# Down-projection operands of a Strassen-style product, made one at a time, in a two-layer encoder kernel

## The chip, the cores and the metric

The kernel runs on one core of a Trainium2 chip. The metric is device time in microseconds (us) of one execution; times of several executions are summed up by their median. The engines that matter are TensorE (PE, matmuls), VectorE (DVE), ScalarE (ACT), GpSimd (POOL) and SyncE (SP), whose queue issues most transfers from HBM.

## The reference, cut to what matters

Two request groups of 512 tokens with 1024 features (float32) go through two layers with shared weights. Each layer is an attention block with four kinds of heads and then a gated MLP with 2816 hidden features. The part at hand is the end of the MLP:

```
u = h @ w_up
up = jnp.pad(u, ((0, 0), (1, 1), (0, 0)))
u = up[:, :-2] * conv_w[0] + up[:, 1:-1] * conv_w[1] + up[:, 2:] * conv_w[2] + conv_b
val, gate = jnp.split(u, 2, axis=-1)
return (val * jax.nn.silu(gate)) @ w_down
```

The result, times a gate per feature, is added to the residual x. The product with `w_down` (2816 x 1024) for both request groups is the down projection.

## The kernel before, in words

**Precision.** Every float32 product is made of three matmuls (`mm3`, L162 to L164). An operand is split into a high half, a rounded copy that ACT makes (L1082), and a low half, operand minus high half, a 128x512 subtract of two SBUF operands (L1078 through `minus`, on DVE or POOL). In the trace the high halves of weights are tiles `whi`, the low halves `wlo`; those of activations are `hh` and `hl`. The pool `hp` has 16 buffers `hh` and 16 `hl`; in the down projection these buffers also hold the raw gated activations as they come from HBM (`g_raw`: `hh` for request group 0, `hl` for request group 1).

**Seven products in place of eight.** The hidden features are 22 chunks of 128 (f = 0 to 21). The down projection takes them in groups of 2n chunks, with n = 3, 3, 3 in layer 0 (`P['gr']`; its last four chunks are multiplied plainly) and n = 4, 3, 4 in layer 1. A group is a 2x2 block product (halves of the features, halves of the output columns, two request groups), done by a Strassen-Winograd scheme with seven products. Each is n x 4 x 3 matmuls: 36 for n = 3, 48 for n = 4. We call them P1 to P7, and a group "first", "second", "third" within its layer. P1 and P2 take raw blocks, P3 to P7 combinations. For each of the n pairs of chunks, `w_combos` makes four sums or differences of weight blocks and `g_combos` four of activation blocks, so 24 of them for n = 3 and 32 for n = 4, and each operand of each product is split, seven weight and seven activation splits for each pair. The temporaries `s1` and `t1` take buffers of the tag `td`, 6 in layer 0 and 8 in layer 1, which is exactly one group's need; they are read last by the split for P4.

**Order.** Both helpers are Python generators. For each product the loop calls `next` on every one of them, then emits the product's matmuls. The third call, ahead of P3, made all four combinations of a pair at once. The compiler orders the instructions of each engine by this order as priority and by its own estimate of when operands are ready; on the chip each engine then takes its list strictly in order. After each product four `add_x` instructions on DVE (L1290) add a PSUM bank to x.

**Who does what.** Strings in `P` give the engine, 'v' for DVE and 'p' for POOL, in turn. `'dl': 'vvp'` are the low halves in the down projection, one in three on POOL. `'ds'` and `'db'`, both 'p', are the weight and activation combinations of all groups but a layer's first; `'d0': 'v'` and `'d1': 'p'` those of the first.

**Weights in flight.** `down_raw` loads one chunk of `w_down` (512 KB) into a ring of buffers: `fr` (letter x, 4 in layer 0, 6 in layer 1, shared with the up projection) and then `fs` (letter d, 3, in memory that is freed when the up projection's temporaries are gone), so 7 and 9 buffers. A group wants 6 or 8 chunks. `sa` is a ring of buffers of the same size (4 in layer 0, 2 in layer 1) for modulation weights, used only up to the end of the up projection.

The up projection uses the same scheme and the same `w_combos`, with other engine keys (`'us'` on POOL, `'ul'` on DVE).

Of the kernel before, what the change touches and what calls it, by code (L numbers as in the profile page):

```python
# [8 lines left out]
F32 = mybir.dt.float32  # L9
# [16 lines left out]
EPS = 1e-6  # L26


P = {'w0': 2.41, 'w1': 2.07, 'b0': 1.49, 'j0': 1.86, 'j1': 1.0, 'p0': 1.06, 'p1': 0.83, 'v': 0.29, 'vd': 0.32, 'f': 0.13, 'fc': 1.16, 'm0': 2.02, 'm1': -0.42, 'o0': 0.58, 'o1': 0.68, 'o2': 0.44, 'a0': 0.66, 'a1': 3.46, 'S': 7, 'K': 6, 'R': 2, 'e': 'p', 'q': 'aa', 'r': 'pv', 'pd': 0.07, 's': -0.28, 'we': 'vvp', 'x': [4, 5, 6, 7, 13, 15, 17, 19], 'hl': 'vpvpvvvv', 'ul': 'v', 'us': 'p', 'ug': 'p', 'uc': 'v', 'uf': 'p', 'tb': 'vpv', 'tl': 'vvvp', 'ds': 'p', 'db': 'p', 'dl': 'vvp', 'ft': [9, 10], 'td': [6, 8], 'fr': [4, 6], 'fs': 3, 'na': 6, 'n1': 2, 'n2': 2, 'gr': [[3, 3, 3], [4, 3, 4]], 'd0': 'v', 'd1': 'p', 't0': 4, 't1': 25, 'sa': [4, 2], 'at': [3.2, 21.2], 'ag': [[4, 4, 0], []]}
UNITS = ['C0', 'D0', 'C2', 'A0', 'D1', 'C1', 'B1', 'A1', 'B0']  # L30
CHUNK = {"A0": 0, "A1": 1, "B0": 2, "B1": 3, "C0": 4, "C1": 5, "C2": 6, "D0": 7, "D1": 8}
GSCALE = {"A": 64 ** -0.5, "B": 64 ** -0.5, "C": 64 ** -0.5, "D": 32 ** -0.5}
# [36 lines left out]

XPOS = P['x']  # L70

# [5 lines left out]
def trunk_kernel(tc, xT, cT, w_ada, w_adac, b_ada, norm_g, w_in, w_out, w_out2, w_out9, w_up, w_down, conv, qkn, rpb,  # L77
                 amask, t5, onehot, tmask, sink, lam_d, subln, blk, ident_in, out):
    nc = tc.nc
    with ExitStack() as ctx:  # L80
# [55 lines left out]
        class Weights:  # L136
# [10 lines left out]
            def split(self, s, cols):  # L147
                hi = self.pool.tile([128, self.width], F32R, name="whi", tag="whi", bufs=self.ring)
                lo = self.pool.tile([128, self.width], F32R, name="wlo", tag="wlo", bufs=self.ring)
                nc.scalar.activation(hi[:, :cols], s[:, :cols], AF.Copy)  # L150
                self.count += 1
                self.eng[self.count % len(self.eng)].tensor_tensor(lo[:, :cols], s[:, :cols], hi[:, :cols].bitcast(F32), op=ALU.subtract)  # L152
                return hi, lo
# [157 lines left out]
        with tc.tile_pool(name="pa", bufs=1, reuse_waits="tile") as pa, \  # L311
# [6 lines left out]
            e = px.tile([128, KC, NG], F32, name="e_c", bufs=1)  # L318
# [57 lines left out]
            for g in range(NG):  # L376
# [3 lines left out]
                for k in range(KC):  # L380
                    hi = hp.tile([128, T], F32R, name="hh", tag="hh")
                    lo = hp.tile([128, T], F32R, name="hl", tag="hl")
# [61 lines left out]
        for l in range(DEPTH):  # L444
# [3 lines left out]
            with ExitStack() as at_ctx:  # L448
# [592 lines left out]
                o0, o1 = outproj(0), outproj(1)  # L1041
# [18 lines left out]
            with ExitStack() as ff_ctx:  # L1060
                fx = ff_ctx.enter_context(tc.tile_pool(name=f"fx{l}", bufs=1, reuse_waits="tile"))
                raws = lambda: fx.tile([128, 1024], F32, name="fr", tag="fr", bufs=P['fr'][l])
# [14 lines left out]
                def minus(key, o, a, b):  # L1077
                    pick(key).tensor_tensor(o, a, b, op=ALU.subtract)  # L1078
# [12 lines left out]
                def w_split(key, s, extra=False):  # L1091

                    blocks, c = [], 0
                    if extra:
                        return quarters(split(key, s, tuple(fx.tile([128, T], F32R, name=n, tag=n, bufs=1)
                                                            for n in ("xhi", "xlo"))))
                    while c < T:
                        if not tail:
                            tail.extend([tuple(W.pool.tile([128, W.width], F32R, name=n, tag=n, bufs=W.ring)
                                               for n in ("whi", "wlo")), 0])  # L1100
                        t, o = tail
                        n = min(T - c, W.width - o)
                        tail.clear()
                        if o + n < W.width:
                            tail.extend([t, o + n])
                        p = split(key, s[:, c:c + n], tuple(x[:, o:o + n] for x in t))
                        blocks += [tuple(x[:, i:i + 128] for x in p) for i in range(0, n, 128)]
                        c += n
                    return blocks

                def w_combos(key, lo, a, tmp):

                    a11, a12, a21, a22 = a
                    yield w_split(lo, a11)
                    yield w_split(lo, a12)
                    s1 = tmp("s1")
                    plus(key, s1, a21, a22)
                    minus(key, a21, a11, a21)
                    minus(key, a11, s1, a11)
                    minus(key, a12, a12, a11)  # L1120
                    for s in (a11, s1, a21, a12, a22):
                        yield w_split(lo, s)

                mm_last[0] = None

# [27 lines left out]
                sa_tile = lambda: fx.tile([128, D], F32, name="sa", tag="sa", bufs=P['sa'][l])  # L1153
# [10 lines left out]
                t0, t1 = P['at']  # L1164
# [18 lines left out]
                with tc.tile_pool(name=f"ft{l}", bufs=1, reuse_waits="tile") as fp, \  # L1183
# [3 lines left out]
                    ft = lambda name: fp.tile([128, T], F32, name=name, tag="ft", bufs=P['ft'][l])  # L1187
# [22 lines left out]
                    us = [t[:, j * T:(j + 1) * T] for t in (sa_tile(), sa_tile()) for j in range(2)]  # L1210
# [26 lines left out]
                    for f in range(NC1, NF):  # L1237
# [11 lines left out]
                        s1 = copy(a)  # L1249
# [17 lines left out]
                fd = ff_ctx.enter_context(tc.tile_pool(name=f"fd{l}", bufs=1, reuse_waits="tile"))  # L1267
                nt = lambda name: fd.tile([128, T], F32, name=name, tag="nt", bufs=3)
                td = lambda name: fd.tile([128, T], F32, name=name, tag="td", bufs=P['td'][l])
                rings = itertools.cycle("x" * P['fr'][l] + "d" * P['fs'])  # L1270

                def down_raw(f):
                    s = raws() if next(rings) == "x" else fd.tile([128, 1024], F32, name="fs", tag="fs", bufs=P['fs'])
                    dma(s, w_down[l, :, f * 1024:(f + 1) * 1024])
                    return s

# [7 lines left out]
                def g_pair():  # L1284
                    return tuple(hp.tile([128, T], F32R, name=n, tag=n) for n in ("hh", "hl"))
# [9 lines left out]
                def g_combos(key, lo, b):  # L1295

                    b11, b12, b21, b22 = b
                    yield split(lo, b11, g_pair())
                    yield split(lo, b21, g_pair())
                    t1 = td("t1")  # L1300
                    minus(key, t1, b12, b11)
                    minus(key, b12, b22, b12)
                    minus(key, b11, b22, t1)
                    minus(key, b21, b21, b11)
                    for s in (b11, t1, b12, b22, b21):
                        yield split(lo, s, g_pair())

                def four(k):
                    return [p_mm(), p_sc(), p_mm(), p_sc()] if k % 2 else [p_tp(), p_pp(), p_tp(), p_ov()]
# [2 lines left out]
                for gi, n in enumerate(P['gr'][l]):  # L1312
                    rw, rg = [], []
                    for i in range(n):
                        rw.append(down_raw(f0 + i))
                        rg.append(g_raw(f0 + i))
                    for i in range(n, 2 * n):
                        rw.append(down_raw(f0 + i))
                        rg.append(g_raw(f0 + i))
                    if gi == 0:  # L1320
                        xs = [(fe if g else fd).tile([128, KC, T], F32, name=f"x{g}", bufs=1) for g in range(NG)]
                        for g, j in ((0, 0), (1, 0), (1, 4), (0, 4)):
                            dma(xs[g][:, j:j + 4], x_ap[:, g, j:j + 4])
                    qa = [w_combos('ds' if gi else 'd0', 'dl', (rw[i][:, :512], rw[n + i][:, :512], rw[i][:, 512:], rw[n + i][:, 512:]), td)
                          for i in range(n)]
                    qb = [g_combos('db' if gi else 'd1', 'dl', rg[i] + rg[n + i]) for i in range(n)]
                    a, b = four(gi + 1), four(gi)
                    c = b
                    for bi, (bank, start, outs) in enumerate(((a, True, ((0, 0),)), (b, True, ((0, 0),)), (a, False, ((1, 0),)),
                                              (c, True, ((1, 4),)), (a, False, ((1, 4),)), (c, False, ((1, 0),)),  # L1330
                                              (a, False, ((0, 4),)))):
                        A = [next(q) for q in qa]
                        B = [next(q) for q in qb]
                        with tc.issue_after(mm_last[0]):
                            pairs = [(i, dp) for i in range(n) for dp in range(4)]
                            if l + 1 == DEPTH and bi == 6:
                                pairs.sort(key=lambda p: p[1])
                            for i, dp in pairs:
                                ins = mm3(bank[dp], A[i][dp], B[i], start and i == 0, i == n - 1)
                        mm_last[0] = ins  # L1340
                        for dp in range(4):
                            for g, d0 in outs:
                                add_x(g, d0 + dp, bank[dp])
                                if f0 + 2 * n == NF and bi in (1, 4, 5, 6) and (dp % 2 or bi == 6):
                                    o = slice(d0 + dp - (bi < 6), d0 + dp + 1)
                                    dma(out[:, g, o], xs[g][:, o])
                    f0 += 2 * n
# [3 lines left out]
                for f in range(f0, NF):  # L1351
                    s = down_raw(f)
# [128 lines left out]
```

## Time and profile before

| what | us |
|---|---|
| median of 3 runs | 2802.25 (2798.87 to 2803.78) |
| the profiled execution | 2799.13 |
| its span, first to last instruction | 2797.3 |
| PE busy in the span | 2610.4 |

The span is 1.8 us shorter than that execution's own time; the rest lies around it. PE's ends are modelled, so its busy time is no measure of full speed; the argument goes by the starts of matmuls and by how long a stage lasts against the number of its matmuls. The down projection begins at about 1209.6 us (layer 0) and 2544.9 us (layer 1) of the span.

### The profile page before, as it was taken

How to read it: one execution, taken by the hardware profiler on the slowest of the kernel's cores; microseconds unless marked ns; L12 is line 12 of the kernel's file. 1: busy time of each engine (PE TensorE's matmuls, PEld its weight loads, DVE VectorE, ACT ScalarE, POOL GpSimd, SP SyncE). 2: the span in 40 equal slices, each digit the busy share in tenths (PEclk: the TensorE clock that was granted, in tenths of full speed). 3: DMA queues.
4: the chain of work that ended last, by engine and by line, in shares of the span. 5: the costliest groups of instructions: out<-in, count | busy, mean ns of one | idle time of the engine just before them, and what ended most of it. 6: DMA issues, size and time to landing. Idle time of an engine off the chain costs nothing. (4 is left out here: it accounts for less than half of the span.)

```text
span 2797.3 us, 39805 instructions
## 1 busy us (share of the span) xinstructions
PE 2610.4 (93%) x13612; PEld 2207.7 (79%) x13612; DVE 2066.3 (74%) x4004; ACT 1393.3 (50%) x2970; POOL 1217.5 (44%) x877
## 2 busy tenths in 40 slices
PE   8899999999789999989898999999996999997989
PEld 4779999878667777767688999998775888886867
DVE  6677578765887777799755776877469777778886
ACT  4456466564444454444334555656544555554432
POOL 2411212255644344378852122122566344436785
PEclk9999999999989999999999999999998999998999
DMA  7744435555144444352223244345550222224321
GB/s 263 207 109 108 123 99 145 144 180 181 61 167 135 143 148 140 116 201 101 82 96 87 78 117 131 103 121 140 180 187 31 76 83 87 72 91 173 106 98 61
DMA packets 146436, 347.71 MB, mean 124 GB/s; under 512 B 21372, under 2 KB 27260, under 8 KB 144952
## 3 DMA queue, kind: packets, MB, share of 16 engines
q1 hardware_dynamic: 133560, 322.08, 37.6%
q10 hardware_dynamic: 12672, 23.07, 2.2%
q8 instruction: 108, 1.77, 0.3%
q14 instruction: 96, 0.79, 0.1%
HBM read 241.19 MB, written 59.51 MB: 107 GB/s over the span
## 5 line engine op out<-in xcount | busy, mean ns | idle before, releaser
L152 POOL TENSOR_TENSOR wlo<-s,whi 128x768 fp32r<-128x768 f32 (+1 forms) x131 | 241.3, 1850 | 390.9 <-ACT whi L150 355.7
L162 PE MATMUL ps_mm<-hh,whi 128*128 128x512 f32 x868 | 345.4, 400 | 50.2 <-ACT t L1141 14.2
L162 PE MATMUL ps_mm<-whi,hh 128*128 128x384 f32 (+1 forms) x1104 | 367.7, 335 | 1.2 <-DVE V L527 1.2
L163 PE MATMUL ps_mm<-wlo,hh 128*128 128x384 f32 (+1 forms) x1104 | 365.3, 331 | 1.8 <-POOL wlo L152 1.8
L164 PE MATMUL ps_mm<-whi,hl 128*128 128x384 f32 (+1 forms) x1104 | 363.1, 330 | 0.0
L164 PE MATMUL ps_mm<-hh,wlo 128*128 128x512 f32 x868 | 343.4, 396 | 14.7 <-POOL wlo L1078 14.7
L163 PE MATMUL ps_mm<-hl,whi 128*128 128x512 f32 x868 | 344.5, 397 | 12.6 <-DVE hl L1078 11.0
L1078 DVE TENSOR_TENSOR wlo<-fr,whi 128x512 fp32r<-128x512 f32 (+1 forms) x393 | 318.0, 824 | 40.4 <-ACT whi L1082 36.5
L1082 ACT ACTIVATE whi<-fr 128x256 fp32r<-128x256 f32 (+1 forms) x448 | 214.8, 517 | 206.4 <-PE ps_mm L163 61.4
L1150 POOL TENSOR_TENSOR t<-t 128x512 f32<-128x512 f32 x88 | 122.2, 1389 | 374.2 <-DVE t L1144 107.9
L162 PEld LDWEIGHTS ps_mm<-whi,hh 128*128 128x128 f32 x1104 | 245.2, 223 | 5.1 <-DVE V L527 3.0
L163 PEld LDWEIGHTS ps_mm<-wlo,hh 128*128 128x128 f32 x1104 | 245.5, 222 | 3.6 <-POOL wlo L152 2.4
L164 PEld LDWEIGHTS ps_mm<-whi,hl 128*128 128x128 f32 x1104 | 245.8, 223 | 1.0
L162 PEld LDWEIGHTS ps_mm<-hh,whi 128*128 128x128 f32 x868 | 164.9, 190 | 95.8 <-ACT t L1141 14.5
L164 PEld LDWEIGHTS ps_mm<-hh,wlo 128*128 128x128 f32 x868 | 165.3, 190 | 51.0 <-POOL wlo L1078 17.2
L163 PEld LDWEIGHTS ps_mm<-hl,whi 128*128 128x128 f32 x868 | 165.1, 190 | 48.0 <-DVE hl L1078 12.4
L625 DVE CUSTOM_DVE_ANT_0 S<-ps_sc,bias 128x512 f32<-128x512 f32 (+3 forms) x288 | 150.0, 529 | 65.3 <-PE ps_sc L716 32.0
L150 ACT ACTIVATE whi<-s 128x768 fp32r<-128x768 f32 (+1 forms) x153 | 123.4, 815 | 124.8 <-DMA s<-in_w_ada 31.0
L573 POOL TENSOR_TENSOR raw<-raw,rs_y 128x512 f32<-128x512 f32 (+1 forms) x36 | 46.5, 1291 | 311.5 <-DVE rs_y L133 228.4
L1141 ACT ACTIVATE t<-u,cw 128x512 f32<-128x512 f32 x120 | 97.7, 814 | 127.7 <-DVE u L1075 112.7
L162 PE MATMUL ps_sc<-hh,whi 128*128 128x512 f32 x404 | 160.1, 396 | 0.0
L164 PE MATMUL ps_sc<-hh,wlo 128*128 128x512 f32 x404 | 159.3, 394 | 0.0
(334 smaller groups left out, 7063.2 us busy)
## 6 DMA issues: line engine op xcount, KB each, us to landing
fr<-in_w_up SPq DMA_DIRECT2D x88, 512.0 KB, 3.5
sa<-in_w_adac SPq DMA_DIRECT2D x56, 512.0 KB, 5.9
s<-in_w_in SPq DMA_DIRECT2D x64, 384.0 KB, 3.4
g_sp<-t ACTq DMA_DIRECT2D x88, 256.0 KB, 2.5
stk<-pr_h SPq DMA_DIRECT2D x152, 128.0 KB, 2.3
stk<-pr_l SPq DMA_DIRECT2D x152, 128.0 KB, 2.6
s<-in_w_ada SPq DMA_DIRECT2D x50, 384.0 KB, 5.4
s<-in_w_out SPq DMA_DIRECT2D x40, 384.0 KB, 3.3
```

What stands on the lines that cost most here:

```text
L150: nc.scalar.activation(hi[:, :cols], s[:, :cols], AF.Copy)
L152: self.eng[self.count % len(self.eng)].tensor_tensor(lo[:, :cols], s[:, :cols], hi[:, :cols].bitcast(F32), op=ALU.subtract)
L162: nc.tensor.matmul(out_, a[0], b[0], start=start, stop=False, skip_group_check=True)
L163: nc.tensor.matmul(out_, a[0], b[1], start=False, stop=False, skip_group_check=True)
L164: return nc.tensor.matmul(out_, a[1], b[0], start=False, stop=stop, skip_group_check=True).ins
L573: (nc.gpsimd if P['r'][i // 2] == 'p' else nc.vector).tensor_tensor(rv, rv, r[:, i * n:(i + 2) * n].rearrange("p (i h) -> p i h", i=2)[:, ...
L625: nc.vector.tensor_tensor_reduce(s[:, :n], p, b, 1.0, init, op0=ALU.add, op1=ALU.min, accum_out=mn)
L1078: pick(key).tensor_tensor(o, a, b, op=ALU.subtract)
L1082: nc.scalar.activation(hi, s, AF.Copy)
L1141: nc.scalar.activation(t, p, AF.Identity, scale=c4[:, 1:2], bias=c4[:, 3:4])
L1150: pick('ug').tensor_tensor(a, a, b, op=ALU.mult)
```

## The change

Three things. First, `w_combos` and `g_combos` make each combination in the call whose product needs it: two of the four ahead of P3, one weight and one activation combination ahead of P5, one weight combination ahead of P6 and one activation combination ahead of P7. The third weight combination is written from the finished second one (a22 - a11 in place of a11 - a21, the same values in exact arithmetic). Second, in the first group of each layer all combinations and low halves are on DVE: in `P`, `'d1'` goes from 'p' to 'v', and a new key `'d2': 'v'` takes the place of `'dl'` there. Third, the ring of raw down weights also takes the `sa` buffers, between `fr` and `fs`: 11 buffers in both layers. The up projection gets the new order of `w_combos` too.

```
                     yield w_split(lo, a12)
                     s1 = tmp("s1")
                     plus(key, s1, a21, a22)
-                    minus(key, a21, a11, a21)
                     minus(key, a11, s1, a11)
+                    yield w_split(lo, a11)
+                    yield w_split(lo, s1)
+                    minus(key, a21, a22, a11)
+                    yield w_split(lo, a21)
                     minus(key, a12, a12, a11)
-                    for s in (a11, s1, a21, a12, a22):
-                        yield w_split(lo, s)
+                    yield w_split(lo, a12)
+                    yield w_split(lo, a22)
...
-                rings = itertools.cycle("x" * P['fr'][l] + "d" * P['fs'])
+                rings = itertools.cycle("x" * P['fr'][l] + "s" * P['sa'][l] + "d" * P['fs'])
 
                 def down_raw(f):
-                    s = raws() if next(rings) == "x" else fd.tile([128, 1024], F32, name="fs", tag="fs", bufs=P['fs'])
+                    ring = next(rings)
+                    s = (raws() if ring == "x" else sa_tile() if ring == "s" else
+                         fd.tile([128, 1024], F32, name="fs", tag="fs", bufs=P['fs']))
...
                     t1 = td("t1")
                     minus(key, t1, b12, b11)
+                    minus(key, b11, b22, t1)
+                    yield split(lo, b11, g_pair())
+                    yield split(lo, t1, g_pair())
                     minus(key, b12, b22, b12)
-                    minus(key, b11, b22, t1)
+                    yield split(lo, b12, g_pair())
+                    yield split(lo, b22, g_pair())
                     minus(key, b21, b21, b11)
-                    for s in (b11, t1, b12, b22, b21):
-                        yield split(lo, s, g_pair())
+                    yield split(lo, b21, g_pair())
...
-                    qa = [w_combos('ds' if gi else 'd0', 'dl', (rw[i][:, :512], rw[n + i][:, :512], rw[i][:, 512:], rw[n + i][:, 512:]), td)
+                    qa = [w_combos('ds' if gi else 'd0', 'dl' if gi else 'd2', (rw[i][:, :512], rw[n + i][:, :512], rw[i][:, 512:], rw[n + i][:, 512:]), td)
                           for i in range(n)]
-                    qb = [g_combos('db' if gi else 'd1', 'dl', rg[i] + rg[n + i]) for i in range(n)]
+                    qb = [g_combos('db' if gi else 'd1', 'dl' if gi else 'd2', rg[i] + rg[n + i]) for i in range(n)]
```

## Rows read from the trace of the kernel before

**Rows 1.** The page, busy time (share of the span) and instructions:

```profile
PE 2610.4 (93%) x13612; PEld 2207.7 (79%) x13612; DVE 2066.3 (74%) x4004; ACT 1393.3 (50%) x2970; POOL 1217.5 (44%) x877
```

**Rows 2.** Busy time in stretches: layer 0's up projection, then the six groups:

```profile
core 0: us, PE busy (x) PEld busy (x) DVE busy (x) ACT busy (x) POOL busy (x), PEclk, DMA share, GB/s
830.00:1200.00 370.00, 367.60 (x1842) 284.42 (x1841) 271.33 (x361) 179.45 (x326) 147.29 (x103) 1.00 0.42 141
...
1209.57:1283.44 73.87, 60.65 (x254) 48.39 (x253) 67.18 (x73) 27.39 (x55) 62.63 (x43) 0.91 0.38 135
1283.44:1343.80 60.36, 58.01 (x253) 46.97 (x252) 58.03 (x65) 24.16 (x49) 49.21 (x34) 1.00 0.29 105
1343.80:1407.06 63.26, 53.33 (x217) 41.79 (x216) 46.00 (x55) 25.16 (x50) 50.26 (x38) 0.95 0.20 66
2544.93:2644.37 99.44, 82.89 (x338) 66.44 (x336) 89.29 (x93) 34.95 (x69) 75.81 (x54) 0.88 0.39 138
2644.37:2702.52 58.15, 57.39 (x253) 47.21 (x252) 54.46 (x62) 23.78 (x49) 47.69 (x33) 1.00 0.34 118
2702.52:2797.30 94.78, 81.54 (x337) 65.27 (x335) 61.67 (x64) 26.08 (x52) 63.76 (x45) 0.95 0.12 45
```

**Rows 3.** L1078's subtracts alone, first two groups: length, DVE (x), POOL (x), PEclk, DMA:

```profile
1209.57:1283.44 73.87, 45.99 (x43) 55.94 (x38) 0.91 0.38 135
1283.44:1343.80 60.36, 38.48 (x34) 45.01 (x31) 1.00 0.29 105
```

**Rows 4.** Timeline of PE: start, duration, instruction, idle before and its releaser:

```profile
1209.57 0.39 PE L162 MATMUL ps_mm<-hh,whi 128*128 128x512 f32 x1
...
1232.54 0.80 PE L162 MATMUL ps_mm<-hh,whi 128*128 128x512 f32 x1 [5.72 <-ACT hh L1082]
...
1242.05 0.79 PE L163 MATMUL ps_mm<-hl,whi 128*128 128x512 f32 x1 [5.67 <-DVE hl L1078]
...
1267.12 0.39 PE L162 MATMUL ps_tp<-hh,whi 128*128 128x512 f32 x1
...
1275.28 0.39 PE L162 MATMUL ps_mm<-hh,whi 128*128 128x512 f32 x1
...
1355.60 0.80 PE L164 MATMUL ps_mm<-hh,wlo 128*128 128x512 f32 x1 [4.57 <-POOL wlo L1078]
...
2723.87 0.80 PE L164 MATMUL ps_mm<-hh,wlo 128*128 128x512 f32 x1 [5.62 <-POOL wlo L1078]
...
2793.07 0.39 PE L164 MATMUL ps_sc<-hh,wlo 128*128 128x512 f32 x1
```

**Rows 5.** Timeline of DVE in layer 0's first group:

```profile
1228.15 1.39 DVE L1290 SCALAR_TENSOR_TENSOR x<-ps_sc,mod,x 128x512 f32<-128x512 f32 x2
...
1230.40 1.75 DVE L1078 TENSOR_TENSOR fs<-fs,fr 128x512 f32<-128x512 f32 x1
...
1240.25 1.74 DVE L1078 TENSOR_TENSOR hl<-hh 128x512 fp32r<-128x512 f32 x1
...
1246.96 2.48 DVE L1078 TENSOR_TENSOR hl<-hl,hh 128x512 fp32r<-128x512 f32 x4
```

**Rows 6.** Timeline of POOL, layer 0's first group, then its third:

```profile
1238.08 1.71 POOL L1078 TENSOR_TENSOR hh<-hh 128x512 f32<-128x512 f32 x1
...
1339.55 4.43 POOL L1078 TENSOR_TENSOR t<-hl,hh 128x512 f32<-128x512 f32 x3
...
1353.83 1.72 POOL L1078 TENSOR_TENSOR wlo<-fr,whi 128x512 fp32r<-128x512 f32 x1
```

**Rows 7.** Timeline of SP's queue: when loads of weights and activations were issued:

```profile
1245.91 5.05 SPq L1274 DMA_DIRECT2D fr<-in_w_down  x3
1251.06 1.22 SPq L1281 DMA_DIRECT2D hh<-g_sp  x1
...
1316.79 0.33 SPq L1274 DMA_DIRECT2D fr<-in_w_down  x1
...
2627.83 46.19 SPq L1274 DMA_DIRECT2D fs<-in_w_down  x3
```

More of the change, by code (lines that the diff above doesn't have):

```diff
@@ L26 @@
 EPS = 1e-6
-P = {'w0': 2.41, 'w1': 2.07, 'b0': 1.49, 'j0': 1.86, 'j1': 1.0, 'p0': 1.06, 'p1': 0.83, 'v': 0.29, 'vd': 0.32, 'f': 0.13, 'fc': 1.16, 'm0': 2.02, 'm1': -0.42, 'o0': 0.58, 'o1': 0.68, 'o2': 0.44, 'a0': 0.66, 'a1': 3.46, 'S': 7, 'K': 6, 'R': 2, 'e': 'p', 'q': 'aa', 'r': 'pv', 'pd': 0.07, 's': -0.28, 'we': 'vvp', 'x': [4, 5, 6, 7, 13, 15, 17, 19], 'hl': 'vpvpvvvv', 'ul': 'v', 'us': 'p', 'ug': 'p', 'uc': 'v', 'uf': 'p', 'tb': 'vpv', 'tl': 'vvvp', 'ds': 'p', 'db': 'p', 'dl': 'vvp', 'ft': [9, 10], 'td': [6, 8], 'fr': [4, 6], 'fs': 3, 'na': 6, 'n1': 2, 'n2': 2, 'gr': [[3, 3, 3], [4, 3, 4]], 'd0': 'v', 'd1': 'p', 't0': 4, 't1': 25, 'sa': [4, 2], 'at': [3.2, 21.2], 'ag': [[4, 4, 0], []]}
+P = {'w0': 2.41, 'w1': 2.07, 'b0': 1.49, 'j0': 1.86, 'j1': 1.0, 'p0': 1.06, 'p1': 0.83, 'v': 0.29, 'vd': 0.32, 'f': 0.13, 'fc': 1.16, 'm0': 2.02, 'm1': -0.42, 'o0': 0.58, 'o1': 0.68, 'o2': 0.44, 'a0': 0.66, 'a1': 3.46, 'S': 7, 'K': 6, 'R': 2, 'e': 'p', 'q': 'aa', 'r': 'pv', 'pd': 0.07, 's': -0.28, 'we': 'vvp', 'x': [4, 5, 6, 7, 13, 15, 17, 19], 'hl': 'vpvpvvvv', 'ul': 'v', 'us': 'p', 'ug': 'p', 'uc': 'v', 'uf': 'p', 'tb': 'vpv', 'tl': 'vvvp', 'ds': 'p', 'db': 'p', 'dl': 'vvp', 'd2': 'v', 'ft': [9, 10], 'td': [6, 8], 'fr': [4, 6], 'fs': 3, 'na': 6, 'n1': 2, 'n2': 2, 'gr': [[3, 3, 3], [4, 3, 4]], 'd0': 'v', 'd1': 'v', 't0': 4, 't1': 25, 'sa': [4, 2], 'at': [3.2, 21.2], 'ag': [[4, 4, 0], []]}
 UNITS = ['C0', 'D0', 'C2', 'A0', 'D1', 'C1', 'B1', 'A1', 'B0']
```

## The prediction, as made before the result

> **What bounds the kernel now.** I read the page first: PE is busy 93% of the span, every other engine less [rows 1]. So time can only come from stretches in which PE waits, and I looked for those with a table of short stretches. Layer 0's up projection has none to speak of: PE is busy 367.60 of 370 us [rows 2], so the new order of `w_combos` there has nothing to win, and with POOL busy 147 of 370 us nothing to lose either. The down projection is different. Take the undisturbed product P6 of layer 0's first group: from its first matmul at 1267.12 to that of P7 at 1275.28 are 8.16 us for 36 matmuls [rows 4]. Seven such products are 57.1 us for n = 3; 48 matmuls in the same rate are 10.88 us, and seven are 76.2 us for n = 4. Against the lengths of the groups [rows 2]:
> - layer 0: 73.87, so 16.8 us lost; 60.36, so 3.3 lost; the third row ends where P7 begins, 63.26 against six products, 49.0, so 14.3 lost;
> - layer 1: 99.44, so 23.3 lost; 58.15, so 1.0 lost; the last group from 2702.52 to the last matmul at 2793.07 [rows 2, 4] 90.6, so 14.4 lost.
>
> Together 73 us, 2.6% of the span. The low granted clocks of these rows (0.88 to 0.95) are part of it: PE's clock falls after such waits, and the matmul behind the 5.72 us wait takes 0.80 us in place of 0.39 [rows 4].
>
> What is late? In the first groups P3 waits 5.72 us for ACT's `hh` and 5.67 us more for DVE's `hl` [rows 4]. While that `hl` (at 1240.25) stands in DVE's list, DVE makes `fs`, a weight combination that only P6 needs (at 1230.40) [rows 5], and POOL still makes an `hh` combination that only P7 needs (at 1238.08) [rows 6]. In the third groups it is P1 itself that waits, 4.57 and 5.62 us, for a `wlo` of POOL [rows 4]: three `t` combinations (at 1339.55) that are meant for P3 and P4 ran on POOL before P1's `wlo` at 1353.83 [rows 6]. Both are work for later products that stands ahead of work that is due.
>
> The price of one subtract depends on company. Four on DVE back to back take 2.48 us, 0.62 each; beside a busy POOL one takes 1.74 or 1.75 [rows 5], and POOL's takes 1.7 then [rows 6]. In layer 0's first group DVE's subtracts of L1078 mean 45.99/43 = 1.07 us, in the second 38.48/34 = 1.13 [rows 3]. Two engines side by side finish two subtracts in 1.75 us; DVE alone needs 1.24.
>
> **The change part by part.**
>
> *Order.* No instruction is added or removed; 12 of 24 combinations (16 of 32 in layer 1) no longer stand ahead of P3's splits. In a third group, where they are POOL's at about 1.5 us (4.43 us for three [rows 6]), P3's demand falls by 18 us for n = 3 and 24 for n = 4, and less stands before P1's `wlo` too.
>
> *Ring.* With 7 buffers layer 0's third group gets chunks only when the second group frees its own: their issue is at 1316.79, 27 us before P1 at 1343.80; in layer 1 SP's three `fs` issues stretch over 46.19 us because each waits for a buffer, and the activations are queued behind them [rows 2, 7]. With 11, four of the second group's chunks and most of the third group's find a buffer already freed by the group before last. Third groups: of 14.3 and 14.4 us lost I keep 4 each, as the second groups, whose operands arrive in time, lose 1.0 and 3.3. Bounds: 2, and 10 if only the order helps and POOL stays behind. Gain taken 20.7.
>
> *First group on DVE.* Layer 0: 24 combinations and 42 low halves, less 9 low halves that P1 and P2's activations want before the group starts, are 57 subtracts; at 0.62 they take 35.3 us, and the 28 `add_x` at 0.69 (1.39 for two [rows 5]) 19.5, together 54.8 against PE's 57.1. It fits only without company. POOL is free for the second group's combinations, but not at once: they need `td` buffers that the first group holds until its split for P4, and activations that were issued at 1251.06, after P3 [rows 7]. I let company fall on half of the subtracts at the second group's mean, 1.13, so 28 x 0.51 = 14 us; DVE needs 69, of which the last product's adds and what PE has in hand hide some: lost 8 in place of 16.8. Layer 1: 88 less 12 are 76 subtracts, 47.1 us, and 19.5 of adds; with half in company (19.4) 86 against 76.2: lost 10 in place of 23.3. Bounds: 3 and 3 without company; with 1.13 on all 57 x 1.13 + 19.5 = 84 and 76 x 1.13 + 19.5 = 105, so 27 and 29 lost. Gain taken 22.1. Two chunks of each first group move from `fs` to `sa`, which is free earlier; I count nothing for it, since P2's wait is inside the loss above.
>
> *What is held longer.* `b11` is now read just ahead of P7, not ahead of P3, so n of the 16 `hh` buffers stay taken four products longer. With 8 raw and 4 to a product in layer 1, two products in flight fill all 16, and the second group's `hh` loads come later. They were issued from 1251.06 on, 32 us before that group [rows 7, 2]; I give the second groups 6 and 4 us lost in place of 3.3 and 1.0: a loss of 5.7. Bounds: 0, and 13 more than that (the rival below).
>
> *Sum.* 20.7 + 22.1 - 5.7 = 37 us. The profiled execution took 2799.13, so 2762; the median of the three runs lies 3.1 us above it. I predict 2765.
>
> **The rivals.** Half a dozen us, 0.2% of the time, is about what a measurement of this kernel can tell from no change.
>
> *Nearly all waits go.* Company is rare, the compiler's order puts due work first, and the lower bounds hold: lost 3, 2, 2, 3, 1 and 2, so 13 of 73. Gain 60, about 2742. For it: POOL has no work in a first group until the second one's operands land. Against: DVE's 54.8 us leave 2 us of play.
>
> *The held buffers decide.* The second group's activations land only in P7, then POOL has 12 combinations and some 5 low halves to make, 17 x 1.5 = 26 us, before P3 two products later: 8 us more lost in layer 0 and 6 in layer 1, and the third groups, late in turn, keep 8 and 9. Lost 8, 14, 8, 10, 10 and 9: gain 14, about 2788.
>
> *POOL locks DVE out of the first groups (slower).* If the second group's 38 POOL instructions (24 combinations, 14 low halves) all run beside the first group, they last 38 x 1.74 = 66 us and each delays a DVE subtract. DVE then needs 66 + 19 x 0.62 + 19.5 = 97 us in layer 0 and 66 + 38 x 0.62 + 19.5 = 109 in layer 1; 23 and 10 us more are lost than before. DVE's lag then also stands ahead of the following splits, so of the 21 us of the third groups a small part, say 6, is left, and the second groups give back 4: 23 more, about 2825. It decides against the change once the subtracts of a first group mean over 1.3 us. Against it: the means are 1.07 and 1.13 even where POOL is busy most of the time [rows 3, 2], and the `td` and `hh` buffers hold POOL back.
>
> *DVE is already full (no change).* DVE is busy 67.18 of 73.87 and 89.29 of 99.44 us of the first groups [rows 2]; about 26 and 35 more subtracts at 0.62 would make 83 and 111 us, 9 and 12 worse, which eats the third groups' 21: about 2803. The row of company speaks against it: 43 subtracts that took 45.99 us [rows 3] would take 27 alone, so a large part of that busy time is waiting for POOL. The Trainium skill has a rule that sides with this rival: its page "Perfetto Trace Analysis", section "Identifying the Most-Contended Engine", takes the occupancy of Vector as a fair measure of how near it is to its limit. By that rule the first groups can't take more work and the sum would be that of this rival; by the rows it is 2765, since the same instruction takes 0.62 or 1.75 us.
>
> **How the numbers follow.** My forecast 0.45 (its own range 2750 to 2780), nearly all waits go 0.20, held buffers 0.17, POOL locks DVE 0.10, DVE full 0.08. The first three are faster, the last but one slower: faster 0.82, same 0.08, slower 0.10. The range leaves out the two bad cases and the tail of the good one: 2737 to 2798.
>
> **What would show it.** Right: P3 of both first groups starts within a few us of two products after P1; POOL does next to nothing in the first 25 us of these groups; DVE's subtracts there mean 0.8 to 0.95; the third groups' chunks are issued right after the first group ends, and P1 doesn't wait for `wlo`; the up projections keep their length. Wrong: subtracts that mean over 1.2 in the first groups; PE waits at P3 of a second group behind `hh` loads; third groups that still begin with a wait, since other things than buffers and order held them.

## The result, and the profile after

The changed kernel takes 2773.99 us in the median of 4 runs (2768.85 to 2783.80); the kernel before, beside it on the same chip, 2803.02 us. The ratio is 0.9905, 95% interval 0.9887 to 0.9923: faster, and 9 us above the predicted 2765, inside the range. The profiled execution took 2775.21 us.

The page's busy line hardly moves against [rows 1], except that POOL has 66 instructions less:

```profile
PE 2612.2 (94%) x13612; PEld 2213.7 (80%) x13612; DVE 2087.9 (75%) x4070; ACT 1390.9 (50%) x2970; POOL 1147.1 (41%) x811
```

Busy time by group, in the columns of [rows 2]; the third groups both end here where P7 begins:

```profile
1215.60:1274.74 59.14, 58.07 (x253) 47.09 (x252) 59.14 (x90) 25.90 (x52) 27.08 (x14) 1.00 0.48 170
1274.74:1342.59 67.85, 60.24 (x253) 48.23 (x252) 67.85 (x67) 26.58 (x52) 66.14 (x45) 0.95 0.25 86
1342.59:1396.11 53.52, 51.20 (x217) 41.58 (x216) 53.43 (x62) 23.39 (x47) 42.55 (x30) 0.97 0.14 48
2534.70:2616.69 81.99, 77.42 (x337) 62.79 (x337) 81.99 (x120) 34.05 (x68) 36.23 (x20) 1.00 0.48 167
2616.69:2682.33 65.64, 59.78 (x253) 48.12 (x252) 61.74 (x66) 23.50 (x49) 56.91 (x40) 0.97 0.26 89
2682.33:2758.62 76.29, 68.79 (x289) 55.76 (x288) 55.40 (x60) 25.66 (x52) 52.17 (x38) 0.96 0.07 28
```

The first groups shrank from 73.87 to 59.14 us and from 99.44 to 81.99, and PE's granted clock there rose from 0.91 and 0.88 to 1.00. The second groups grew, from 60.36 to 67.85 and from 58.15 to 65.64. Layer 0's third group went from 63.26 to 53.52; layer 1's from 79.9 to 76.29, counted to P7's start. With the prediction's 8.16 and 10.88 us for a product, the groups lose 2.0, 10.7 and 4.5 us in layer 0 and 5.8, 8.5 and 11.0 in layer 1, 42.5 in place of 73.

The subtracts of L1078 alone, in the columns of [rows 3], for layer 0's three groups:

```profile
1215.60:1274.74 59.14, 40.89 (x60) 13.42 (x9) 1.00 0.48 170
1274.74:1342.59 67.85, 49.71 (x38) 61.66 (x42) 0.95 0.25 86
1342.59:1396.11 53.52, 37.90 (x36) 42.55 (x30) 0.97 0.14 48
```

One subtract on DVE takes 40.89/60 = 0.68 us in the mean in the first group and 49.71/38 = 1.31 in the second (some of them, in both, are 256 columns wide and shorter). Where POOL is away most of the time, DVE works nearly twice as fast.

The longest waits that PE still has, on its timeline, in three of the groups: one of under a microsecond in layer 0's first, one of 5 in its second, and three in layer 1's third:

```profile
1236.04 0.50 PE L163 MATMUL ps_mm<-hl,whi 128*128 128x512 f32 x1 [0.90 <-DVE hl L1078]
...
1304.96 0.79 PE L163 MATMUL ps_tp<-hl,whi 128*128 128x512 f32 x1 [5.03 <-POOL hl L1078]
...
2696.31 0.50 PE L164 MATMUL ps_tp<-hh,wlo 128*128 128x512 f32 x1 [2.49 <-POOL wlo L1078]
2700.67 0.50 PE L163 MATMUL ps_tp<-hl,whi 128*128 128x512 f32 x1 [1.56 <-POOL hl L1078]
2713.03 0.79 PE L164 MATMUL ps_mm<-hh,wlo 128*128 128x512 f32 x1 [3.45 <-POOL wlo L1078]
```

P1 of a third group no longer waits for `wlo` (in layer 1 its P2 and P3 wait for POOL instead, the last three lines), and P3 of a first group no longer waits over 10 us as in [rows 4]. The longest wait is P3's in a second group now, and its releaser is POOL. Over all six groups PE waits 29 us; 17 of them end with an instruction of POOL and 11 with one of DVE. POOL's timeline ahead of that low half (at 1303.19):

```profile
1290.88 2.93 POOL L1078 TENSOR_TENSOR hh<-hh 128x512 f32<-128x512 f32 x2
...
1298.16 1.73 POOL L1078 TENSOR_TENSOR fr<-fr,fs 128x512 f32<-128x512 f32 x1
1299.85 1.71 POOL L1078 TENSOR_TENSOR wlo<-fs,whi 128x512 fp32r<-128x512 f32 x1
1301.52 1.70 POOL L1078 TENSOR_TENSOR hh<-hh 128x512 f32<-128x512 f32 x1
1303.19 1.71 POOL L1078 TENSOR_TENSOR hl<-hh 128x512 fp32r<-128x512 f32 x1
```

The `hh` differences (three of them) are b21 - b11, which only P7 needs, and PE waits for a P3 operand behind them. The compiler fills POOL's list by its own estimate of readiness, so writing them late does not keep them late. Last, SP's queue:

```profile
1237.61 0.80 SPq L1331 DMA_DIRECT2D x<-x_ap  x2
1244.42 7.91 SPq L1279 DMA_DIRECT2D fr<-in_w_down  x3
1254.08 3.04 SPq L1286 DMA_DIRECT2D hh<-g_sp  x4
...
1261.26 0.53 SPq L1279 DMA_DIRECT2D fr<-in_w_down  x1
...
1263.10 1.01 SPq L1279 DMA_DIRECT2D sa<-in_w_down  x2
...
1311.84 0.33 SPq L1279 DMA_DIRECT2D sa<-in_w_down  x1
...
1315.99 0.39 SPq L1286 DMA_DIRECT2D hl<-g_sp  x1
```

The second group's activations are issued 20.7 us ahead of their P1 (32 before [rows 7]). The ring does what it was meant to do for the weights. Counted along its eleven buffers, the first of the three `fr` issues is the second group's last chunk. The two behind it, the `fr` at 1261.26 and the first two `sa` are the third group's, five of its six chunks, issued more than 78 us ahead of its P1 at 1342.59. Before, five of the six were issued from 1316.79 on, 27 us or less ahead [rows 7]. The third group's activations stay late: they follow from 1316 on, 27 us ahead of P1, the lead that they had before.

### The profile page after: what moved, and what is told of

It is laid out like the page before. It is cut to its first block, busy times and chain, and to the rows that moved or that the text cites. A ratio compares the mean times of both kernels' runs of the same rounds, so it can differ in the third digit from the quotient of the medians.

```text
span 2773.4 us, 39721 instructions
## 1 busy us (share of the span) xinstructions
PE 2612.2 (94%) x13612; PEld 2213.7 (80%) x13612; DVE 2087.9 (75%) x4070; ACT 1390.9 (50%) x2970; POOL 1147.1 (41%) x811
## 5 line engine op out<-in xcount | busy, mean ns | idle before, releaser
L1078 DVE TENSOR_TENSOR wlo<-fr,whi 128x512 fp32r<-128x512 f32 (+1 forms) x385 | 313.7, 831 | 36.7 <-ACT whi L1082 28.9
L1153 POOL TENSOR_TENSOR t<-t 128x512 f32<-128x512 f32 x88 | 128.3, 1458 | 428.9 <-DVE t L1147 110.4
L1082 ACT ACTIVATE whi<-fr 128x512 fp32r<-128x512 f32 (+1 forms) x416 | 199.7, 517 | 164.0 <-PE ps_mm L163 64.8
L1145 DVE SCALAR_TENSOR_TENSOR t<-u,cw,t 128x511 f32<-128x511 f32 x120 | 117.8, 981 | 62.9 <-ACT t L1144 62.0
```

Source lines behind the costliest of these rows:

```text
L1082: nc.scalar.activation(hi, s, AF.Copy)
L1145: nc.vector.scalar_tensor_tensor(t[:, 1:], p[:, :T - 1], c4[:, 0:1], t[:, 1:], op0=ALU.mult, op1=ALU.add)
L1153: pick('ug').tensor_tensor(a, a, b, op=ALU.mult)
```

## The experiments

Twelve runs in three sets, r1 to r3. "Lost" is a group's length minus its products at 8.16 or 10.88 us (third groups: six products), as in the prediction. Ratios are to the kernel before, run beside each set (medians 2799.4, 2800.5 and 2800.2 us).

| kernel | median us | ratio, 95% interval | lost, layer 0 | lost, layer 1 | sum |
|---|---|---|---|---|---|
| before, beside the first profile | 2803.0 | 1 | 16.8, 3.3, 14.3 | 23.3, 1.0, 14.4 | 73 |
| changed (first profile) | 2774.0 | 0.9905 [0.9887, 0.9923] | 2.0, 10.7, 4.5 | 5.8, 8.5, 11.0 | 43 |
| r1_again | 2769.3 | 0.9882 [0.9855, 0.9908] | 2.0, 10.7, 4.5 | 5.9, 8.7, 9.9 | 42 |
| r1_old_order | 2770.6 | 0.9892 [0.9864, 0.9921] | 12.0, 5.0, 4.4 | 9.3, 9.5, 2.6 | 43 |
| r1_old_engines | 2789.0 | 0.9965 [0.9949, 0.9982] | 15.6, 4.6, 7.1 | 20.1, 14.0, 5.0 | 66 |
| r1_old_ring | 2781.0 | 0.9932 [0.9910, 0.9953] | 6.8, 12.2, 4.6 | 11.9, 4.0, 14.1 | 54 |
| r2_gate_dve | 2769.4 | 0.9890 [0.9876, 0.9905] | 3.7, 13.3, 1.4 | 6.8, 8.1, 10.0 | 43 |
| r2_b21_early | 2778.0 | 0.9921 [0.9907, 0.9936] | 10.1, 8.0, 5.5 | 6.1, 10.4, 8.0 | 48 |
| r2_hold | 2769.8 | 0.9887 [0.9872, 0.9902] | 2.1, 14.0, 2.4 | 3.3, 7.2, 9.0 | 38 |
| r2_all_dve | 2743.2 | 0.9799 [0.9783, 0.9815] | 1.6, 8.1, 0 | 4.0, 0, 0 | 14 |
| r3_x_queue | 2770.7 | 0.9889 [0.9866, 0.9911] | 4.1, 10.5, 5.5 | 5.7, 8.5, 11.1 | 45 |
| r3_before_all_dve | 2747.5 | 0.9806 [0.9785, 0.9826] | 11.2, 0, 1.2 | 11.8, 0, 0.1 | 24 |
| r3_all_dve_old_order | 2748.8 | 0.9807 [0.9783, 0.9831] | 9.0, 0, 0 | 9.2, 0, 0 | 18 |
| r3_all_dve_x_queue | 2746.0 | 0.9796 [0.9766, 0.9827] | 2.5, 7.6, 0 | 3.3, 0, 0 | 13 |

The losses are read from one execution each. Their sum follows the time to within some 6 us: from before to r2_all_dve 59 us of loss and 57 us of time go.

### The change again, and each part undone

r1_again is the changed kernel once more, as a base for the three others.

> The changed kernel itself, beside which the others of this set are read. Its profile had the first group of layer 0 start 6 us later than in the kernel before, at the same list of instructions up to there. If that is drift from one execution to the next, the start lies elsewhere in this profile (1209 to 1216 us) and the group lengths stay (59, 68, 54 and 82, 66, 91 us within 2 each). If the change causes it, the start is again at 1215 to 1216.

Measured: 2769.3, and the groups have the same lengths within 2 us. Layer 0's first group starts at 1217.4 us, outside both ranges of the expectation. The shift is there before any instruction that the change touches: the up projection's first two copies `whi<-fr` start at 698.32 us in the kernel before, at 704.79 in the changed kernel and at 703.80 here.

**r1_old_order** goes back to the old order in both helpers:

```
-                    minus(key, a11, s1, a11)
-                    yield w_split(lo, a11)
-                    yield w_split(lo, s1)
-                    minus(key, a21, a22, a11)
-                    yield w_split(lo, a21)
+                    minus(key, a21, a11, a21)
+                    minus(key, a11, s1, a11)
                     minus(key, a12, a12, a11)
...
+                    for s in (a11, s1, a21, a12, a22):
+                        yield w_split(lo, s)
```

> The changed kernel with the old order of combinations (all four ahead of P3); engines and ring stay new. Theory that the parts act in separate places: DVE alone then makes 24 (32) combinations ahead of P3, 15 (20) us of them, and P3 of the first groups waits some 5 and 9 us; the third groups start again with a wait on POOL; together 12 to 20 us over the changed kernel, about 2790. Rival, order does nearly all: the first groups are as long as before (74 and 99) and the time is 2800. Rival, order does nothing since the compiler orders by its own estimates: within 4 us of the changed kernel.

Measured: 0.9892 against 0.9882, no difference. That is the time of the last rival, but not its mechanism, since the groups do change. Layer 0's first two groups and layer 1's third in this kernel:

```profile
1217.62:1286.73 69.11, 60.30 (x253) 48.58 (x252) 69.11 (x95) 26.25 (x52) 43.18 (x24) 0.93 0.42 145
1286.73:1348.86 62.13, 59.22 (x254) 48.28 (x252) 60.73 (x63) 23.70 (x48) 54.52 (x39) 0.97 0.27 94
...
2694.42:2762.37 67.95, 65.60 (x289) 53.98 (x288) 52.32 (x60) 25.60 (x52) 44.93 (x33) 1.00 0.08 31
```

The new order saves 10.0 us in layer 0's first group (69.1 to 59.1), then gives back 5.7 in the second; in layer 1 it saves 3.5 in the first and gives back 8.3 in the third. It moves a wait to a later group. (Beside r1_again in place of the first profile, layer 1's third group gives back 7.2.)

**r1_old_engines** has the first groups' POOL work back:

```
-'d2': 'v', ... 'd1': 'v'
+'d1': 'p'
-... 'dl' if gi else 'd2' ...
+... 'dl' ...
```

> The changed kernel with the old engines in the first groups (activation combinations and one low half in three on POOL); order and ring stay new. Theory that DVE without company makes the first groups: their subtracts on DVE mean about 1.1 us again in place of 0.68, the groups take some 68 and 92 us in place of 59 and 82, second groups get back a part (POOL's last gate product is not held up), together 8 to 16 us over the changed kernel. Rival, the order alone did it: first groups within 3 us of the changed kernel's.

Measured: 2789.0, so the move to DVE is worth some 20 us of the change, more than the 8 to 16 expected, and the first groups lose nearly what they lost before, 15.6 and 20.1 us. L1078's subtracts in layer 0's first group, in the columns of [rows 3], mean 49.66/41 = 1.21 us on DVE again:

```profile
1215.28:1287.95 72.67, 49.66 (x41) 54.98 (x36) 0.93 0.39 137
```

**r1_old_ring** takes the `sa` buffers out of the ring:

```
-                rings = itertools.cycle("x" * P['fr'][l] + "s" * P['sa'][l] + "d" * P['fs'])
+                rings = itertools.cycle("x" * P['fr'][l] + "d" * P['fs'])
```

> The changed kernel with the old ring of 7 and 9 weight buffers; order and engines stay new. Theory that the ring makes the weights early: the third groups' chunks are issued within 30 us of their first product again, and the third groups, now 54 and 91 us, get 5 to 10 us longer each; in the first group P2 waits for the chunks in fs. 10 to 18 us over the changed kernel. Rival, the activations' 16 buffers are the gate, not the weights: within 4 us of the changed kernel.

Measured: 2781.0, so the ring is worth some 12 us, only in part where it was expected. Layer 0's third group loses 4.6 us with the old ring and 4.5 with the new, though its chunks come late again; layer 1's third loses 14.1 against 9.9. The larger part is in the first groups (6.8 and 11.9 against 2.0 and 5.9). With the old ring layer 0's first group has its last two chunks issued some 9 us before it starts at 1210.34, with the new one some 37 us before it starts at 1215.60. The old ring's issue, its subtracts in that group, and the new ring's issue:

```profile
1200.79 0.81 SPq L1277 DMA_DIRECT2D fs<-in_w_down  x2
...
1210.34:1274.29 63.95, 45.73 (x68) 10.53 (x7) 0.95 0.43 155
...
1178.36 0.88 SPq L1279 DMA_DIRECT2D sa<-in_w_down  x2
```

One subtract still means 45.73/68 = 0.67 us, but 68 of them fall inside the group in place of 60. That fits chunks that came too late for their low halves to be made ahead of the group.

### Why are the second groups late?

Four causes were on the table: POOL's slow gate products hold the loads up, `b11` is held too long, the compiler's order on POOL, or simply POOL's amount of work beside DVE.

**r2_gate_dve**

```
-                    pick('ug').tensor_tensor(a, a, b, op=ALU.mult)
+                    (nc.vector if f == NF - 1 else pick('ug')).tensor_tensor(a, a, b, op=ALU.mult)
```

> The changed kernel with the last up chunk's gate product on DVE in place of POOL. Theory 'POOL is starved, so the transfers come late': in the changed kernel POOL's last gate products take 5.80 and 3.48 us beside DVE's dense stream, the store of the gate waits for them, the residual's load waits for the store, and SP's queue hands out the second group's activation loads only 20.7 us ahead of their group (32 us before the change). With the product on DVE the loads of layer 0 are issued some 8 to 15 us earlier, and the second group of layer 0 shortens from 67.9 to 60 to 63 us, that of layer 1 from 65.7 by some 2 to 4; the first groups become longer by at most 2 us each; in all 2760 to 2767. Rival 'the loads are in time anyway, POOL's own work in the second groups is what is late': the loads move, the second groups stay within 1 us, and the time stays at 2768 to 2776.

Measured: no change, and no test of the theory. The second of the two gate products now waits in DVE's list instead, until 1229.8, 20.0 us after the group's start; the residual's load is issued 22.9 us after that start, no earlier than the 22.0 of the changed kernel.

**r2_b21_early** makes `minus(key, b21, b21, b11)` right behind t1's split.

> The changed kernel with b21 - b11 made right behind t1's split, so that b11's buffer is not held until P7. Theory 'held buffers': the second group's activation loads are issued some 8 us earlier and the second groups shorten by 3 to 6 us each, in all 2763 to 2769. Rival 'the loads wait in SP's queue behind the residual's load, not for buffers': their issue moves by under 2 us in layer 0, the second groups stay within 1.5 us, and the time stays at 2769 to 2776. The one combination that DVE makes earlier in the first groups costs P5 at most 2 us in either case.

Measured: 2778.0, slower than the changed kernel. The loads do come earlier (34.8 us after the group's start against 38.5), 32.4 us ahead of their P1 again as in the kernel before, and layer 0's second group gains 2.7 us. But its first group grows by 8.1: DVE has three subtracts more to make ahead of P5, and POOL's first combination comes 39.2 us after the start in place of 45.7, so there is more company (L1078 on DVE means 49.45/63 = 0.78 us in place of 0.68). The held `b11` thus explains the late loads of layer 0's second group, but the late loads explain at most a small part of its loss.

**r2_hold** queues POOL's combinations for P5 to P7 behind its own last low half for P3:

```
+                    with tc.issue_after(hold[0]) if behind and e is nc.gpsimd and hold[0] else nullcontext():
+                        ins = e.tensor_tensor(o, a, b, op=ALU.subtract).ins
```

> The changed kernel with the combinations that P5 to P7 need queued on POOL behind POOL's own low halves for P3 (the compiler otherwise puts up to some ten of them ahead of such a low half). Theory 'POOL's order': the waits of the second group of layer 0 at P3 (5.03 us) and of the third group of layer 1 (2.49, 1.56 and 3.45 us) fall to under 1.5 us each; the groups shorten by 4 to 7 us each, in all 2758 to 2766. Rival 'POOL's amount': the work is only moved, P5 to P7 wait in place of P3, and the groups stay within 2 us: 2768 to 2777.

Measured: 2769.8, no difference. P3's 5.03 us wait in layer 0's second group is gone, but 7.6 us of waits for DVE's `add_x` stand in its place, and the group loses 14.0 us; in layer 1's third group one wait replaces three of 7.5 us together:

```profile
2699.42 0.80 PE L164 MATMUL ps_tp<-hh,wlo 128*128 128x512 f32 x1 [6.61 <-POOL wlo L1082]
```

So the order on POOL only chooses which product waits.

**r2_all_dve** takes POOL out of all groups, keys alone:

```
-'ds': 'p', 'db': 'p', 'dl': 'vvp'
+'ds': 'v', 'db': 'v', 'dl': 'v'
```

> The changed kernel with all combinations and low halves of all groups of the down projections on DVE, none on POOL. Theory 'the pair is worth no more than DVE alone, company sets the price': a group of n = 3 is 66 subtracts at 0.62 to 0.68 and 28 adds at 0.69, 60 to 64 us, one of n = 4 74 to 79; the second groups come to 60 to 63 us, the third ones to 6 products in 50 to 53 us, and the time to 2755 to 2766; subtracts mean at most 0.72 us throughout. Rival 'DVE becomes the bound': with no second engine DVE falls behind PE in each second and third group, these become 70 us or longer, and the time is 2780 or more.

Measured: 2743.2, below the 2755 to 2766 of the theory and 26 us below r2_gate_dve and r2_hold of the same set, which run like the changed kernel. Groups, then L1078's subtracts in layer 0's:

```profile
1213.95:1272.62 58.67, 57.74 (x254) 47.14 (x252) 58.67 (x100) 25.86 (x52) 9.29 (x2) 1.00 0.49 170
1272.62:1337.80 65.18, 60.60 (x253) 49.22 (x252) 65.18 (x113) 26.31 (x52) 0.00 (x0) 0.95 0.28 89
1337.80:1386.76 48.96, 48.96 (x217) 40.54 (x216) 48.64 (x85) 23.16 (x46) 0.00 (x0) 1.00 0.10 33
2523.91:2604.09 80.18, 78.04 (x337) 64.16 (x336) 80.18 (x136) 34.20 (x67) 2.90 (x2) 0.98 0.48 171
2604.09:2661.22 57.13, 57.13 (x254) 47.30 (x253) 57.13 (x100) 24.81 (x50) 0.00 (x0) 1.00 0.30 102
2661.22:2726.49 65.27, 65.27 (x289) 54.05 (x288) 60.25 (x105) 25.68 (x52) 0.00 (x0) 1.00 0.08 33
...
1213.95:1272.62 58.67, 38.23 (x66) 0.00 (x0) 1.00 0.49 170
1272.62:1337.80 65.18, 45.74 (x81) 0.00 (x0) 0.95 0.28 89
1337.80:1386.76 48.96, 33.55 (x60) 0.00 (x0) 1.00 0.10 33
```

Three of six groups run at PE's pace, 48.96, 57.13 and 65.27 us. Summed over the six groups, DVE makes 452 subtracts in 253.9 us; in the changed kernel DVE spent 270.7 us on 292 of them while POOL spent 243.6 us on 170. POOL's help cost DVE more time than it saved. The edit also takes away every wait for POOL's own, slower list (17 of the 29 us above), and the runs don't part the two effects.

### Is the rest of the change needed, then?

**r3_before_all_dve** is the kernel before, old order and old ring, with only the keys set to 'v' (`'ds'`, `'db'`, `'dl'`, `'d1'`).

> The kernel before the change (old order, old ring) with all combinations and low halves of the down projections on DVE. Theory 'company is the whole loss': it reaches 2740 to 2752, as the changed kernel with all of them on DVE does (2743), since a third group without POOL has little for buffers or order to mend. Rival 'order and buffers are needed beside it': P3's waits in the first groups (about 10 us in each layer) and the late chunks of layer 0's third group (half a dozen us or more) stay, and it comes to 2758 to 2775.

Measured: 2747.5, the ratio's interval overlapping that of r2_all_dve. One line of the kernel before gives some 1.7 times the gain of the whole change (52.7 us against the 30.1 of r1_again). Its groups in layer 0:

```profile
1209.98:1278.24 68.26, 61.22 (x254) 49.51 (x252) 67.51 (x114) 27.00 (x54) 3.13 (x2) 0.95 0.41 146
1278.24:1335.36 57.12, 57.12 (x254) 47.30 (x252) 57.12 (x99) 24.83 (x50) 0.00 (x0) 1.00 0.34 111
1335.36:1385.54 50.18, 49.26 (x218) 40.46 (x216) 50.18 (x88) 24.89 (x50) 0.00 (x0) 1.00 0.23 74
```

The third group loses 1.2 us in place of 14.3 with the old ring and the old order. P3's waits in the first group are still there.

**r3_all_dve_old_order** is r2_all_dve with the old order (the diff of r1_old_order).

> The changed kernel with all combinations and low halves of the down projections on DVE, but in the old order. With POOL at work the order was worth nothing in sum (2770.6 against 2769.3): it gained some 13 us in the first groups and gave them back later. Theory 'it was given back to POOL's work': on DVE alone the old order puts P4 to P7's combinations ahead of P3's splits again, P3 of each first group waits some 8 to 10 us, nothing is given back, and the time is 2752 to 2765. Rival 'DVE has the same total to do, so P3's wait is caught up later': within 5 us of the new order, 2740 to 2748.

Measured: 2748.8, not told apart from r2_all_dve by the ratios (0.9807 and 0.9799). Its first two groups in layer 0:

```profile
1212.59:1278.66 66.07, 60.06 (x253) 48.46 (x252) 66.07 (x112) 26.34 (x53) 9.44 (x2) 0.95 0.45 152
1278.66:1335.78 57.12, 57.12 (x253) 47.30 (x252) 57.12 (x100) 23.84 (x48) 0.00 (x0) 1.00 0.30 102
```

Together 123.2 us for 212 DVE instructions; with the new order 58.67 + 65.18 = 123.9 us for 213. DVE is busy without a gap in both, so P3's wait in the first group becomes P3's wait in the second. In layer 1 the first group gains 5.2 us by the new order and nothing is given back.

**r3_x_queue and r3_all_dve_x_queue** move residual loads to POOL's queue, in the changed kernel and in r2_all_dve:

```
-                            dma(xs[g][:, j:j + 4], x_ap[:, g, j:j + 4])
+                            (dma2 if j else dma)(xs[g][:, j:j + 4], x_ap[:, g, j:j + 4])
```

> The changed kernel with the last two residual loads of each layer issued from POOL's queue in place of SP's. Moving the gate product to DVE had not moved these loads (22.9 us after the first group's start against 22.0), so it did not test this. Theory 'SP's queue': the loads wait some 21 us for the gate's store, and the second group's activation loads stand behind them; without them the activations are issued at least 8 us earlier (under 31 us after the start of layer 0's first group, where the changed kernel has 38.5), POOL begins the second group's combinations that much earlier, the second groups shorten by 4 to 8 us in layer 0 and 2 to 6 in layer 1, 2757 to 2765 in all. Rival 'POOL and DVE together are full': the loads move but POOL's earlier work lengthens the first groups (subtracts of DVE there 0.8 us or more in the mean) by what the second ones gain, and the time stays at 2766 to 2774.

> The changed kernel with all combinations and low halves on DVE and the last two residual loads of each layer on POOL's queue, which has nothing else to do there. Theory 'DVE is the bound of what is left': DVE is busy 100% of layer 0's first two groups in the kernel with all on DVE, so earlier operands win nothing: 2740 to 2746, second group of layer 0 within 2 us of 65.2. Rival 'the rest of the waits are late loads': the second group's 3.9 us wait at P3 goes, and it falls to 2733 to 2739.

Measured: 2770.7 and 2746.0, no difference to their bases. The edit missed what it aimed at: the load that waits is the first half of request group 1, which stayed on SP (at 1232.55, 23.8 us after the group's start), and the activations were issued 40.5 us after the start against 38.5. Whether earlier loads would help the changed kernel's second groups stays open.

## Why the prediction was right, and which of its steps were not

**The bound.** Right: all the time came from the waits in the down projections, and PE is again busy for 367.60 of 370 us of layer 0's up projection.

**The sum** was 37 us, and by groups 30.6 were gained: 32.3 in the first groups, 13.2 in the third, and 14.9 lost in the second. The profiled executions differ by 23.9; 6.0 of the rest is layer 0's down projection starting at 1215.60 in place of 1209.57. That start lies between 1208.8 and 1222.7 in the profiles of the runs, and the shift is there before the first instruction that the change touches (see r1_again), so I take it for spread.

**"First group on DVE"** was the right mechanism, mis-sized downwards: 2.0 and 5.8 us lost in place of 8 and 10, 32.3 us gained where I took 22.1. Two terms failed. "Company on half of the subtracts" is one: they mean 0.68 us against the (35.3 + 14.3)/57 = 0.87 that the term assumes. POOL has 14 instructions there, none of them subtracts until 1261, since the second group's activations land only then. That r1_old_engines puts nearly the whole loss back, at 1.21 us a subtract, shows that the engines are what matters. The ring is the other: "I count nothing" for the two chunks that move from `fs` to `sa`, but the old ring costs the first groups 4.8 and 6.0 us, as much as the whole gain beyond the forecast. With the old ring they lose 6.8 and 11.9, close to my 8 and 10, but at 0.67 us a subtract, so without the company from which I had worked these out: more subtracts fall inside the group (68 in place of 60 in layer 0). That agreement is luck.

**"Third groups", 4 us lost each,** held in layer 0 (4.5) and not in layer 1 (11.0, and 9.9 in r1_again, at the bound of 10). The reason given doesn't carry it. The ring does bring layer 0's chunks earlier, but the old ring changes that group by 0.1 us; in layer 1 it is worth 4.2. The order gains nothing there: with the old one the third groups lose 4.4 and 2.6, and on POOL the compiler's own order overrules it. No part undone alone brings back layer 0's 14.3 us (4.4, 7.1 and 4.6), so which of them together took it away stays open, and the 4 came true by luck. What the runs do show is that the third groups lack DVE and POOL time: without POOL they lose 0 and 0, and 1.2 and 0.1 even with old ring and old order. One row was also misread: of the three `fs` issues that "stretch over 46.19 us" in layer 1, the first two went out at 2627.83 and 2630.23, and only the third came 43 us later, at 2673.68.

**"What is held longer", 6 and 4 us,** measured 10.7 and 8.5. The mechanism was right for the loads, which are late in layer 0 because `b11` is held, but not for the loss: freeing `b11` early gave back only 2.7 us in layer 0 and none in layer 1. In layer 0 the new order leaves more of the work for the second group, which loses 5.0 with the old order and 8.1 even without POOL; with POOL a subtract costs 1.31 us there beside POOL's 1.47. In layer 1 the old order changes nothing (9.5), and without POOL the loss is 0.

**The rivals.** "Nearly all waits go" at 2742 is what r2_all_dve does: its condition, company is rare, was met by the change in the first groups alone. "POOL locks DVE out of the first groups" did not come, because POOL starts late. It came in layer 0's second one, at 1.31 us, the mark that I had set for the first.

"DVE is already full" was wrong: the first group's DVE was 91% busy with 73 instructions in 73.87 us [rows 2], and after the change it did 90 in 59.14. So the occupancy rule of the Trainium skill, page "Perfetto Trace Analysis", section "Identifying the Most-Contended Engine", misled here, since busy time held waiting for POOL. The same page of the Trainium skill, section "Optimizing Scalar/DVE Operations", says that work passed between Vector and GpSimd may gain nothing, because they share a read port into SBUF. The traces agree: 452 subtracts in 253.9 us on DVE alone against 270.7 for 292 with POOL's help. They show the price of company, not the port itself.

## What to carry to other kernels

Before two engines are balanced, measure what one costs beside the other and alone: where an instruction takes 0.62 us alone and 1.75 in company, handing work to the second engine slows the pair, and its busy share alone doesn't tell its room. Try the change that takes the slow helper away first; order and buffers may then need no mending. An order written into the code moves a wait rather than removing it when the engine has no gap left: compare sums over neighbouring groups, not the one group that got shorter.

## What was not expected of the hardware

POOL's price in company is not always the 1.7 us of [rows 6]. While DVE runs back to back, one 128x512 product of two SBUF operands on POOL lasts 5.80 us by the profile, and DVE beside it keeps its pace, three subtracts in 1.89 us. POOL's timeline, then DVE's, in the changed kernel:

```profile
1221.08 5.80 POOL L1153 TENSOR_TENSOR t<-t 128x512 f32<-128x512 f32 x1 [19.42 <-DVE t L1147]
...
1220.84 1.89 DVE L1078 TENSOR_TENSOR fr<-s,fr 128x512 f32<-128x512 f32 x3
1222.64 0.68 DVE L1078 TENSOR_TENSOR hh<-hl,t 128x512 f32<-128x512 f32 x1
1223.24 0.68 DVE L1078 TENSOR_TENSOR hl<-hl 128x512 f32<-128x512 f32 x1
```

The same pair thus has two patterns: both slow to 1.7 us, or DVE at full pace and POOL shut out for several of its instructions. What selects between them, the runs don't show; spans on POOL are rough, so its 5.80 us is to be read as an order of size.
